# An encoder step on one core: norms from an all-ones product with roots on whole rows, and a written order for VectorE and ScalarE at the end

## The chip, the cores and the metric

The kernel runs on one core of a Trainium2 chip. The metric is device time in microseconds, and less is better. The core has a matrix engine (TensorE, PE in the profile, with its weight loads shown as PEld), VectorE (DVE), ScalarE (ACT), GpSimd (POOL) and a sync engine (SP) that issues transfers. TensorE writes its results to PSUM, from which VectorE and ScalarE read them. All other data of the kernel is in SBUF, as tiles of 128 partitions by some columns.

## What is computed

One inference step of a two-layer encoder over 512 prompt frames and 64 frames of a running stream, 576 tokens of 1024 features. Layer 0 mixes tokens by causal averages over 2 to 16 frames, layer 1 by sparse attention. Behind each mixer stands a perceptron (1024 to 4096 and back) with a squared ReLU. A root-mean-square norm stands ahead of each of these four parts, and one more at the end. Cut to what matters here:

```python
def _rmsnorm(x, g):
    xf = x.astype(jnp.float32)
    xf = xf * lax.rsqrt(jnp.mean(xf * xf, axis=-1, keepdims=True) + EPS)
    return (xf * g.astype(jnp.float32)).astype(x.dtype)

def _mlp(h, w_up, w_down):
    u = jax.nn.relu(h @ w_up)
    return (u * u) @ w_down

for i in range(DEPTH):
    h = _rmsnorm(x, norm_mix[i])
    ...
    x = x + y.astype(x.dtype)
    x = x + _mlp(_rmsnorm(x, norm_mlp[i]), w_up[i], w_down[i])
return _rmsnorm(x, norm_final)
```

## The kernel before, in words

**Layout.** The residual x lies transposed: eight tiles of 128 features (partitions) by 576 tokens (columns). A token's sum of squares therefore runs across partitions and across tiles. The 576 columns are two halves of 288 (`HT`). float32 products are made of two-part splits: every operand is an upper part and a lower part, and three products stand for one. The weights are split in the same way: a raw weight arrives by DMA, ScalarE casts it to the upper part `wh` (line 184), VectorE subtracts to get the lower part `wl` (line 185). One such pair is a unit of 512 columns; units lie in a ring of slots, and a cast into a slot waits until TensorE has read the slot's old content. `next_block` (line 248) asks for units some four to six ahead of their use.

**A perceptron's start.** `split_x` scales and splits x by the norm's gain, without the root, and `Norm.add` sums the squares of the eight tiles into `s2` (128 by 576). The up projection runs in blocks of 128 outputs (`project`, line 264): 48 products of 288 columns each, into a pair of PSUM banks. There are two such pairs. Since the root is a factor per token, it is applied when a block is read out: `activated` (line 373) takes max(block, 0) times `norm.rb`, the root spread over all partitions, into `v`. So the first two blocks need no norm; it has to be there before the fourth block can have the first block's banks. After the second block come the sums: `stats` (line 292) multiplies s2, 128 tokens at a time (the last time 64), with two columns of ones, so that token sums land one per partition, five columns in all, and `rms_steps` (line 330) turns them into inverse roots: a root on ScalarE, a reciprocal on VectorE, and one Newton step in three operations. During the third block (which has two single banks of its own) `spread` (line 297) puts them on all partitions: `diagonals` multiplies the identity with them on VectorE, a product with the all-ones block `ones` at k = 5 (`SPREAD_AT`) makes every partition hold every token's value in `rb`, and ScalarE copies that to `rbm` in SBUF (line 303). Then come the v's of the first two blocks (line 379).

**The end.** `last` (line 539) does the last two output tiles of the last perceptron (tiles 6 and 7) with plain products, one half of the tokens after the other, and puts the final norm beside them. `finish` (line 546) is a generator: token sums and roots, then the diagonal and its product, then the copy for GpSimd (which scales tiles 4 and 5), and then the scalings of all tiles (line 567) with the output DMAs. For the first half it is advanced at the feature steps 4, 11 and 13 (`NORM_STEPS`) of the second half's 16; for the second half it runs behind the last product. The second half's work on tiles 6 and 7 is an add to x (line 589), a square on ScalarE (line 591), and for tile 6 an add to the sum (line 593).

**What sets the order.** Each engine runs its own queue in order. Almost everywhere a scheduler of the framework orders each queue by its own model of the times; nothing in the code says when a `wl` comes relative to a `v`. Inside `tc.manual_schedule` (line 581) the engines named keep the order in which the code is written: before, TensorE alone. A semaphore holds an instruction until what it needs is there, and everything behind it on the same engine waits too.

Of the kernel before, what the change touches and what calls it, by code (L numbers as in the profile page):

```python
# [9 lines left out]
F32 = mybir.dt.float32  # L10
F32R = mybir.dt.float32r
AF = mybir.ActivationFunctionType
ALU = mybir.AluOpType
ENG = mybir.EngineType
PSUM = bass.MemoryType.PSUM

P = 128
D = 1024
KT = D // P
TP = 512  # L20
TS = 64
T = TP + TS
HT = T // 2
# [7 lines left out]
WARM = 16  # L31
LAST = 2
FINAL_ASIDE = ((4, 5), (4, 5))
NORM_STEPS = (4, 11, 13)
PACE = (1, 2, 2)
PACED = 3 * NIDX - 1
SLOTS = {"xs": 8, "a": 3, "b": 3, "c": 3, "d": 3, "e": 2}
HEADS = {"a": 512, "c": 1024, "d": 1024}
UNITS = (6, 2)
UNDER = 64  # L40
SPREAD_AT = 5
SPARE_UNITS = 6
RAWS = (2, 2)
MLP_BLOCKS = ("up", "even", "odd", "down")
# [6 lines left out]
def pool_dsa_kernel(ctx: ExitStack, tc: tile.TileContext, a, o):  # L51
# [30 lines left out]
    def slot(tag, s, dt=F32R):  # L82
        if tag == "x":
            return resid.tile([P, SLOT], dt, tag=tag, name=uid(s))
        n = HEADS.get(tag, SLOT) if "cst2" in phase else SLOT
        return phase["xs" if tag == "xs" else "slots"].tile([P, n], dt, tag=tag, bufs=SLOTS[tag], name=uid(s))
# [15 lines left out]
    def psum1(s="po"):  # L102
        return phase["po"].tile([P, 512], F32, tag="po", name=uid(s))
# [4 lines left out]
    def halves(t):  # L108
        return t.rearrange("p (h t) -> p h t", h=2)
# [154 lines left out]
    def project(pt, w, xs, between=iter(()), cols=((0, HT), (HT, HT))):  # L264

        n = len(xs)
        for k in range(n):
            next(between, None)
            wh, wl = at(w, k)
            for i, (wt, part) in enumerate(((wh, 0), (wh, 1), (wl, 0))):  # L270
                for h, (c, m) in enumerate(cols):
                    pe.matmul(  # L272
                        pt[h][:, :m] if isinstance(pt, tuple) else pt[:, h, :m], wt, xs[k][:, part, c:c + m],
                        start=(k == 0 and i == 0), stop=(k == n - 1 and i == 2),
                    )

    class Norm:
# [14 lines left out]
        def stats(self):  # L292
            pt = psum1("st")
            token_sums(pt, self.s2)
            self.r = rms(pt)

        def spread(self):
            diag = diagonals(self.r)
            self.rb = tmp("rb" + self.s, "rb", 1)
            for h in range(2):  # L300
                pb = psum1("rb")
                pe.matmul(pb[:, :HT], ones, diag[:, h * HT:(h + 1) * HT], start=True, stop=True)
                act.copy(self.rb[:, h * HT:(h + 1) * HT], pb[:, :HT])
            return self.rb

    def diagonals(r, n=T, diag=None):

        diag = tmp("diag") if diag is None else diag
        c, rest = n // P, n % P
        idb = ident.rearrange("p (o c) -> p o c", o=1)  # L310
        rc = r.rearrange("p (o c) -> p o c", c=1)
        dve.tensor_tensor(diag[:, :c * P].rearrange("p (i c) -> p i c", c=P), idb.to_broadcast([P, c, P]),
                          rc[:, :c].to_broadcast([P, c, P]), ALU.mult)
        if rest:
            dve.tensor_scalar(diag[:, c * P:n], ident[:, :rest], r[:, c:], None, ALU.mult)
        return diag

    def token_sums(pt, *sums, n=T):
        for i in range(0, n, P):
            m = min(P, n - i)  # L320
            for s2 in sums:
                pe.matmul(pt[:m, i // 64:i // 64 + 2], s2[:, i:i + m], ones[:, 0:2], start=s2 is sums[0], stop=s2 is sums[-1])

    def rms(pt, n=T):

        steps = rms_steps(pt, n)
        next(steps)
        return next(steps)

    def rms_steps(pt, n=T, early=False):  # L330
        c, rest = n // P, n % P
        ms, rt, t, r = (small(c + (rest > 0), s + str(n)) for s in ("ms", "rt", "nt", "r"))
        ends = [(P, slice(0, c), slice(0, 2 * c, 2))]
        if rest:
            dve.memset(ms[:, c:], 1.0)
            dve.memset(rt[:, c:], 1.0)
            ends.append((rest, slice(c, c + 1), slice(2 * c, 2 * c + 1)))
        if early:
            yield
        for rows, to, at in ends:  # L340
            act.activation(rt[:rows, to], pt[:rows, at], AF.Sqrt, scale=1.0 / D, bias=eps[:rows])
        for rows, to, at in ends:
            dve.tensor_scalar(ms[:rows, to], pt[:rows, at], 1.0 / D, EPS, ALU.mult, ALU.add)
        yield
        dve.reciprocal(r, rt)
        dve.scalar_tensor_tensor(t, r, -0.5, r, ALU.mult, ALU.mult)
        dve.tensor_tensor(t, t, ms, ALU.mult)
        dve.scalar_tensor_tensor(r, t, 1.5, r, ALU.add, ALU.mult)
        yield r
# [13 lines left out]
    def mlp(layer, gi, late=0, end=None):  # L363
# [127 lines left out]

        v = early = None

        def spread():

            for k in range(KT):
                if k == SPREAD_AT:
                    norm.spread()
                yield

        def finished(c, i, pt, us):
            nonlocal v, early
            if i % 2 == 0:
# [15 lines left out]
        for n, (c, i) in enumerate(steps):  # L519
            if i is not None:  # L520
                w = next_block()
                pt = (psum1("up"), psum1("up")) if n == 2 else psum("up")
                project(pt, w, xs, spread() if n == 2 else iter(()))
                todo.append((c, i, pt, us[c]))
                if n == 0:
                    continue
                if n == 1:
                    norm.stats()
                    continue
                for t in todo:  # L530
                    finished(*t)
                todo.clear()
                continue
            down(c, us[c])
# [4 lines left out]
    def last(parts):  # L539

        norm = Norm("f", lambda: slot("xs", "sq", F32)[:, :T])
        for k in range(KT - LAST):
            norm.add(k)
        ws = [next_block() for _ in range(LAST)]

        def finish(c, n, aside, rest):
            t = slice(c, c + n)
            room = halves(slot("xs", "room", F32))
            for k in aside:
                act.activation(x[k][:, t], x[k][:, t], AF.Copy, scale=gv[:, 4, k:k + 1])  # L550
            st = psum1("st")
            token_sums(st, norm.s2[:, t], rest, n=n)
            r = rms(st, n)
            yield
            diag = diagonals(r, n, room[:, 0])
            pb = psum1("rb")
            pe.matmul(pb[:, :n], ones, diag[:, :n], start=True, stop=True)
            yield
            if aside:
                rb = room[:, 1, :n]  # L560
                act.copy(rb, pb[:, :n])
            yield
            for k in range(KT):
                if k in aside:
                    pool.tensor_tensor(x[k][:, t], x[k][:, t], rb, ALU.mult)
                else:
                    dve.scalar_tensor_tensor(x[k][:, t], x[k][:, t], gv[:, 4, k:k + 1], pb[:, :n], ALU.mult, ALU.mult)
                if c and k > 3:
                    (nc.sync if k % 2 else act).dma_start(o["y"][:, k, t], x[k][:, t])
                elif k % 2:  # L570
                    nc.sync.dma_start(o["y"][:, k - 1:k + 1, t], x.t[k // 2][:, :, t])

        def during(steps):

            for k in range(LAST * KT):
                if k in NORM_STEPS:
                    next(steps)
                yield

        before = between = iter(())  # L580
        with tc.manual_schedule(engines={ENG.PE}):
            for c, n, us in ((0, HT, parts[0]), (HT, HT, parts[1])):
                t = slice(c, c + n)
                s2 = norm.s2[:, t]
                for j in range(LAST):
                    k = KT - LAST + j
                    pt = psum("dn")
                    project(pt, ws[j], us, between, cols=((0, n),))
                    dve.tensor_tensor(x[k][:, t], x[k][:, t], pt[:, 0, :n], ALU.add)
                    sq = norm.room()[:, :n]  # L590
                    act.activation(sq, x[k][:, t], AF.Square)
                    if j < LAST - 1:
                        dve.tensor_tensor(s2, s2, sq, ALU.add)
                for _ in before:
                    pass
                before = finish(c, n, FINAL_ASIDE[c > 0], sq)
                between = during(before)
            for _ in before:
                pass
# [735 lines left out]
```

## Time and profile before

| what | value |
|---|---|
| median of 3 runs (lowest to highest) | 1113.73 us (1112.39 to 1115.95) |
| span of the profiled execution, first to last instruction | 1114.1 us |
| busy share of TensorE, VectorE, ScalarE, GpSimd | 98%, 74%, 48%, 27% |
| mean granted TensorE clock | 0.991 |
| first and second perceptron: token sums start | 56.4 us, 724.0 us |
| end: first half's sums start; last six scalings start | 1092.3 us, 1106.6 us |

Profile rows are read like this: start and duration in us, engine, line, operation, output tile <- input tiles, shape, count, and in brackets how long the engine sat idle before, and what ended that. A product of plain float32 operands shows as two entries, so "x4" at line 302 is two products. The span of 1114.1 us is 0.4 above the median of the runs.

### The profile page before, as it was taken

The numbers are of one execution on the slowest core, as the hardware profiler recorded it, in microseconds if no ns is written. First come the engines' busy times: TensorE is split into PE (matmuls) and PEld (weight loads), VectorE is DVE, ScalarE is ACT, GpSimd is POOL, SyncE is SP. The second block draws the span as 40 slices with busy tenths as digits, with TensorE's granted clock in tenths as the row PEclk, the third lists the DMA queues.
The fourth block names the chain that finished last, engine by engine and source line by source line (L and its number), as shares of the span: only waits on it lengthen the run. The fifth ranks groups of instructions, "written<-read, shape, count | busy, mean of one in ns | idle before, by whom it ended". The sixth has DMA issues, their size and how long they took to land.

```text
span 1114.1 us, 21065 instructions
## 1 busy us (share of the span) xinstructions
PE 1090.9 (98%) x8222; PEld 1077.3 (97%) x8222; DVE 825.7 (74%) x1562; ACT 539.0 (48%) x983; POOL 305.1 (27%) x260
## 2 busy tenths in 40 slices
PE   8999999999999999999899999999999999999995
PEld 8999999999999999999889999999999999999995
DVE  7867856866786797779799954767757866766884
ACT  8545434434434454443387665545434434434541
POOL 3312201302221261227682430012211302231331
PEclk8999999999999999999999999999999999999997
DMA  6433542554365345446742443643643554365212
GB/s 218 138 104 77 160 135 77 122 162 114 86 161 142 77 128 178 117 150 178 204 115 66 137 116 112 173 117 77 161 133 85 123 153 114 86 164 140 57 39 85
DMA packets 60610, 138.72 MB, mean 125 GB/s; under 512 B 9969, under 2 KB 21536, under 8 KB 60512
## 3 DMA queue, kind: packets, MB, share of 16 engines
q1 hardware_dynamic: 46544, 103.50, 30.4%
q0 software_dynamic: 8928, 16.26, 9.2%
q10 hardware_dynamic: 5040, 17.63, 5.2%
q8 instruction: 65, 1.06, 0.4%
q14 instruction: 33, 0.27, 0.1%
HBM read 122.28 MB, written 10.89 MB: 120 GB/s over the span
## 4 chain that ended last, share of the span: by engine, by line
PE 82%; DVE 10%; DMA 3%; ACT 1%; issue 1%; SPq 1%; POOL 0%; DVEq 0%; ACTq 0%; POOLq 0%
PE up L272 37%; PE b L439 13%; PE c L439 8%; PE a L439 8%; PE wo L272 3%; PE pj L272 2%; DVE work L1016 2%; DVE m L1015 2%; DMA raw<-in_w_in 2%; PE o L1091 2%; PE z L702 2%; PE pb L807 1%; PE wa L272 1%; DVE wl L185 1%; PE dn L272 1%
## 5 line engine op out<-in xcount | busy, mean ns | idle before, releaser
L272 PE MATMUL up<-xs,wh 128*128 128x288 f32 x2048 | 355.5, 295 | 0.0
L184 ACT CAST wh<-raw 128x512 fp32r<-128x512 f32 (+1 forms) x316 | 194.1, 620 | 303.2 <-PE up L272 130.6
L272 PEld LDWEIGHTS up<-xs,wh 128*128 128x128 f32 x2048 | 299.6, 188 | 0.6 <-DVE v L379 0.4
L185 DVE TENSOR_TENSOR wl<-raw,wh 128x512 fp32r<-128x512 f32 (+1 forms) x292 | 235.6, 810 | 63.6 <-ACT wh L184 58.6
L272 PE MATMUL up<-xs,wl 128*128 128x288 f32 x1024 | 218.6, 295 | 0.0
L272 PEld LDWEIGHTS up<-xs,wl 128*128 128x128 f32 x1024 | 164.0, 188 | 0.0
L439 PE MATMUL b<-u,wh 128*128 128x288 f32 x744 | 150.1, 295 | 0.2 <-DVE x L484 0.2
L439 PEld LDWEIGHTS b<-u,wh 128*128 128x128 f32 x744 | 119.0, 188 | 0.5 <-DVE x L484 0.5
L226 POOL TENSOR_TENSOR sum<-sum,raw 128x512 f32<-128x512 f32 x31 | 52.9, 1708 | 241.3 <-DMA raw<-in_w_down 187.9
L184 ACT CAST wh<-sum 128x512 fp32r<-128x512 f32 x93 | 56.9, 620 | 110.1 <-PE up L272 42.8
L439 PE MATMUL b<-u,wl 128*128 128x288 f32 x372 | 109.0, 295 | 0.0
L439 PE MATMUL a<-u,wh 128*128 128x288 f32 x496 | 101.2, 295 | 0.0
L439 PE MATMUL c<-u,wh 128*128 128x288 f32 x496 | 100.4, 295 | 0.0
L379 DVE SCALAR_TENSOR_TENSOR v<-up,rbm 128x576 f32<-128x576 f32 x60 | 45.2, 756 | 66.7 <-PE up L272 62.4
L185 DVE TENSOR_TENSOR wl<-sum,wh 128x512 fp32r<-128x512 f32 x93 | 76.9, 830 | 7.6 <-ACT wh L184 6.3
L439 PEld LDWEIGHTS a<-u,wh 128*128 128x128 f32 x496 | 79.6, 188 | 0.0
L439 PEld LDWEIGHTS c<-u,wh 128*128 128x128 f32 x496 | 79.3, 188 | 0.1
L209 POOL DMA_DIRECT2D raw<-in_w_down x31 | 26.8, 866 | 185.0 <-DMA raw<-in_w_down 89.3
L439 PE MATMUL a<-u,wl 128*128 128x288 f32 x248 | 73.2, 296 | 0.1
L439 PE MATMUL c<-u,wl 128*128 128x288 f32 x248 | 73.0, 294 | 0.0
L439 PEld LDWEIGHTS b<-u,wl 128*128 128x128 f32 x372 | 69.7, 188 | 0.0
L208 POOL DMA_DIRECT2D sum<-in_w_down x31 | 28.4, 934 | 141.4 <-DVE wl L185 85.1
(246 smaller groups left out, 2010.0 us busy)
## 6 DMA issues: line engine op xcount, KB each, us to landing
raw<-in_w_up SPq DMA_DIRECT2D x64, 512.0 KB, 3.8
raw<-in_w_down SPq DMA_DIRECT2D x64, 512.0 KB, 3.6
raw<-in_w_o ACTq DMA_DIRECT2D x16, 512.0 KB, 3.8
sum<-in_w_down SPq DMA_DIRECT2D x31, 256.0 KB, 3.9
sum<-in_w_down POOLq DMA_DIRECT2D x31, 256.0 KB, 5.2
raw<-in_w_down POOLq DMA_DIRECT2D x31, 256.0 KB, 4.1
raw<-in_w_in ACTq DMA_DIRECT2D x15, 512.0 KB, 4.4
q<-st SPq DMA_DIRECT2D x32, 144.0 KB, 2.5
```

The costliest lines, as they stand in the source:

```text
L184: act.copy(h, src)
L185: how["sub"].tensor_tensor(l, src, f32(h), ALU.subtract)
L208: pool.dma_start(s1, odd[:, 512:], accum_op=ALU.add)
L209: pool.dma_start(raw[:, :512], even[:, :512], accum_op=ALU.add)
L226: pool.tensor_tensor(s2, s1, a11, ALU.add)
L272: pe.matmul(pt[h][:, :m] if isinstance(pt, tuple) else pt[:, h, :m], wt, xs[k][:, part, c:c + m], start=(k == 0 and i == 0), stop=(k == n ...
L379: dve.scalar_tensor_tensor(v, pt[:, :, :HT], 0.0, halves(norm.rb), ALU.max, ALU.mult)
L439: pe.matmul(bank[:, :HT], wt, ut, start=first and j == 0 and i == 0, stop=last and j == 3 and i == 2, skip_group_check=True)
L702: pe.matmul(z[s, i][:n, (g % 2) * 256:(g % 2 + 1) * 256], lhs, rhs, start=kk + j == 0, stop=kk == 1 and j == 2)
L1015: dve.max(m8[:np_], wk[:np_])
L1016: dve.match_replace(wk[:np_], m8[:np_], wk[:np_], TAKEN)
L1091: pe.matmul(oc[:, 2 * s + hh], pT[:, c:c + P], V[:, kt, vs], start=kt == 0, stop=kt == i)
```

## The change

In the perceptrons, one function `everywhere` takes the place of `stats` and `spread`. For each half it multiplies the all-ones block with the squares' sum s2, so that every partition gets every token's sum at once, and makes the inverse root on the full 128 by 288 block by `root`: a root on ScalarE, then on VectorE a reciprocal and three operations of the Newton step. There are no diagonal, no second product and no copy. It is called behind the second block, where `stats` was. The generator that put the spread into the third block goes.

The last norm does the same on each half (two products into one bank, s2 and the last square), at step 4; the root lies in PSUM, where the scalings read it. The scalings of the first half are written in three parts: tiles 0 and 1 with the root, 2 to 5 at step 8, 6 and 7 behind the second half's last add. The gain scalings of GpSimd's tiles move behind the root on ScalarE. And in this last part VectorE and ScalarE, too, keep the written order. The norm ahead of the attention stays as it was; `rms_steps` and `diagonals` only lose a parameter (not shown).

```diff
-NORM_STEPS = (4, 11, 13)
+NORM_STEPS = (4, 8)
-SPREAD_AT = 5
...
+        def everywhere(self):
+            self.rb = tmp("rb" + self.s, "rb", 1)
+            for h in range(2):
+                t = slice(h * HT, (h + 1) * HT)
+                pt = psum1("st")
+                pe.matmul(pt[:, :HT], ones, self.s2[:, t], start=True, stop=True)
+                root(self.rb[:, t], pt[:, :HT], self.rb[:, t], tmp("nt")[:, :HT])
...
+    def root(r, sums, first, t):
+        act.activation(t, sums, AF.Sqrt, scale=1.0 / D, bias=eps)
+        dve.reciprocal(first, t)
+        dve.scalar_tensor_tensor(t, first, -0.5 / D, first, ALU.mult, ALU.mult)
+        dve.scalar_tensor_tensor(t, sums, D * EPS, t, ALU.add, ALU.mult)
+        dve.scalar_tensor_tensor(r, t, 1.5, first, ALU.add, ALU.mult)
...
-                project(pt, w, xs, spread() if n == 2 else iter(()))
+                project(pt, w, xs)
...
-                    norm.stats()
+                    norm.everywhere()
...
         def finish(c, n, aside, rest):
             t = slice(c, c + n)
-            room = halves(slot("xs", "room", F32))
+            room = slot("xs", "room", F32)
+            first, spare, rb = (room[:, i * n:(i + 1) * n] for i in range(3))
+            pb = psum1("rb")
+            pe.matmul(pb[:, :n], ones, norm.s2[:, t], start=True, stop=False)
+            pe.matmul(pb[:, :n], ones, rest, start=False, stop=True)
+            root(pb[:, :n], pb[:, :n], first, spare)
             for k in aside:
                 act.activation(x[k][:, t], x[k][:, t], AF.Copy, scale=gv[:, 4, k:k + 1])
-            st = psum1("st")
-            token_sums(st, norm.s2[:, t], rest, n=n)
-            r = rms(st, n)
-            yield
-            diag = diagonals(r, n, room[:, 0])
-            pb = psum1("rb")
-            pe.matmul(pb[:, :n], ones, diag[:, :n], start=True, stop=True)
-            yield
-            if aside:
-                rb = room[:, 1, :n]
-                act.copy(rb, pb[:, :n])
-            yield
+            act.copy(rb, pb[:, :n])
             for k in range(KT):
+                if k in (2, 6):
+                    yield
                 if k in aside:
                     pool.tensor_tensor(x[k][:, t], x[k][:, t], rb, ALU.mult)
...
-        with tc.manual_schedule(engines={ENG.PE}):
+        with tc.manual_schedule(engines={ENG.PE, ENG.DVE, ENG.Activation}):
```

How this moves the queues, at the places where it matters. VectorE at the first perceptron's start, before (st holds the token sums, r the roots; wl_959 and wl_963 are the subtractions for the two halves of a later block's weights; v is the readout of the first two blocks):

```order
L343 TENSOR_SCALAR ms_128_782<-st_776 128x4
L343 TENSOR_SCALAR ms_128_782<-st_776 64x1
L345 RECIPROCAL r_131_785<-rt_129_783 128x5
L346 SCALAR_TENSOR_TENSOR nt_130_784<-r_131_785 128x5
L347 TENSOR_TENSOR nt_130_784<-nt_130_784,ms_128_782 128x5
L348 SCALAR_TENSOR_TENSOR r_131_785<-nt_130_784,r_131_785 128x5
L312 TENSOR_TENSOR diag_838<-ident,r_131_785 128x512
L315 TENSOR_SCALAR diag_838<-ident,r_131_785 128x64
L185 TENSOR_TENSOR wl_959<-raw_796,wh_958 128x512
L379 SCALAR_TENSOR_TENSOR v_866<-up_678,rbm_140_841 128x576
L379 SCALAR_TENSOR_TENSOR v_866<-up_727,rbm_140_841 128x576
L185 TENSOR_TENSOR wl_963<-raw_796,wh_962 128x512
```

The same place of the changed kernel, where the lines and numbers are a little lower (wl_946 is the old wl_959, wl_950 the old wl_963; nt and rbm are the two halves' roots):

```order
L317 RECIPROCAL rbm_127_776<-nt_779 128x288
L317 RECIPROCAL rbm_127_776<-nt_787 128x288
L318 SCALAR_TENSOR_TENSOR nt_779<-rbm_127_776 128x288
L184 TENSOR_TENSOR wl_946<-raw_793,wh_945 128x512
L318 SCALAR_TENSOR_TENSOR nt_787<-rbm_127_776 128x288
L319 SCALAR_TENSOR_TENSOR nt_779<-st_777,nt_779 128x288
L319 SCALAR_TENSOR_TENSOR nt_787<-st_785,nt_787 128x288
L320 SCALAR_TENSOR_TENSOR rbm_127_776<-nt_779,rbm_127_776 128x288
L320 SCALAR_TENSOR_TENSOR rbm_127_776<-nt_787,rbm_127_776 128x288
L184 TENSOR_TENSOR wl_950<-raw_793,wh_949 128x512
L395 SCALAR_TENSOR_TENSOR v_853<-up_678,rbm_127_776 128x576
L395 SCALAR_TENSOR_TENSOR v_853<-up_727,rbm_127_776 128x576
```

Eight operations on all 288 columns stand where eight smaller ones stood, wl_946 has come in between them, and wl_950, which stood behind the v's, now stands ahead of them. The second perceptron has the same sequence.

VectorE at the end, before (x_8384 is tiles 6 and 7, dn_13030 and dn_13083 the second half's products for them, rb_13095 the first half's root, s the sum of squares):

```order
L348 SCALAR_TENSOR_TENSOR r_2081_13056<-nt_2080_13055,r_2081_13056 128x3
L589 TENSOR_TENSOR x_8384<-x_8384,dn_13030 128x288
L312 TENSOR_TENSOR room_13043<-ident,r_2081_13056 128x256
L315 TENSOR_SCALAR room_13043<-ident,r_2081_13056 128x32
L593 TENSOR_TENSOR s_2065_12954<-s_2065_12954,sq_13080 128x288
L567 SCALAR_TENSOR_TENSOR x_8381<-x_8381,gv,rb_13095 128x288 x2
L567 SCALAR_TENSOR_TENSOR x_8382<-x_8382,gv,rb_13095 128x288 x2
L567 SCALAR_TENSOR_TENSOR x_8384<-x_8384,gv,rb_13095 128x288 x2
L589 TENSOR_TENSOR x_8384<-x_8384,dn_13083 128x288
```

The same place of the changed kernel (x_8371 is tiles 6 and 7, dn_13004 and dn_13048 the products, rb_13018 the first half's root):

```order
L317 RECIPROCAL room_13017<-room_13017 128x288
L318 SCALAR_TENSOR_TENSOR room_13017<-room_13017 128x288
L319 SCALAR_TENSOR_TENSOR room_13017<-rb_13018,room_13017 128x288
L320 SCALAR_TENSOR_TENSOR rb_13018<-room_13017 128x288
L572 SCALAR_TENSOR_TENSOR x_8368<-x_8368,gv,rb_13018 128x288 x2
L594 TENSOR_TENSOR x_8371<-x_8371,dn_13004 128x288
L598 TENSOR_TENSOR s_2057_12928<-s_2057_12928,sq_13045 128x288
L572 SCALAR_TENSOR_TENSOR x_8369<-x_8369,gv,rb_13018 128x288 x2
L594 TENSOR_TENSOR x_8371<-x_8371,dn_13048 128x288
L572 SCALAR_TENSOR_TENSOR x_8371<-x_8371,gv,rb_13018 128x288 x2
```

The add of dn_13004 (tile 6), which stood ahead of the diagonal, now stands behind the whole root and two scalings; the add of dn_13048 (tile 7), which stood behind all six scalings, now stands ahead of the last two.

More of the change, by code (lines that the diff above doesn't have):

```diff
@@ L304, in spread, with diagonals @@
             return self.rb
-    def diagonals(r, n=T, diag=None):
-        diag = tmp("diag") if diag is None else diag
-        c, rest = n // P, n % P
+    def root(r, sums, first, t):
[4 more added lines that the diff above has]
+        dve.scalar_tensor_tensor(r, t, 1.5, first, ALU.add, ALU.mult)
+    def diagonals(r):
+        diag = tmp("diag")
+        c, rest = T // P, T % P
         idb = ident.rearrange("p (o c) -> p o c", o=1)
@@ L314, in diagonals, with token_sums, rms, rms_steps @@
         if rest:
-            dve.tensor_scalar(diag[:, c * P:n], ident[:, :rest], r[:, c:], None, ALU.mult)
+            dve.tensor_scalar(diag[:, c * P:], ident[:, :rest], r[:, c:], None, ALU.mult)
         return diag
-    def token_sums(pt, *sums, n=T):
-        for i in range(0, n, P):
-            m = min(P, n - i)
+    def token_sums(pt, *sums):
+        for i in range(0, T, P):
+            m = min(P, T - i)
             for s2 in sums:
                 pe.matmul(pt[:m, i // 64:i // 64 + 2], s2[:, i:i + m], ones[:, 0:2], start=s2 is sums[0], stop=s2 is sums[-1])
-    def rms(pt, n=T):
-        steps = rms_steps(pt, n)
+    def rms(pt):
+        steps = rms_steps(pt)
         next(steps)
         return next(steps)
-    def rms_steps(pt, n=T, early=False):
-        c, rest = n // P, n % P
-        ms, rt, t, r = (small(c + (rest > 0), s + str(n)) for s in ("ms", "rt", "nt", "r"))
+    def rms_steps(pt, early=False):
+        c, rest = T // P, T % P
+        ms, rt, t, r = (small(c + (rest > 0), s) for s in ("ms", "rt", "nt", "r"))
         ends = [(P, slice(0, c), slice(0, 2 * c, 2))]
@@ L492, in mlp @@
         v = early = None
[L494 to L498, printed above, removed]
-                yield
         def finished(c, i, pt, us):
@@ L547, in finish @@
             t = slice(c, c + n)
-            room = halves(slot("xs", "room", F32))
+            room = slot("xs", "room", F32)
[4 more added lines that the diff above has]
+            root(pb[:, :n], pb[:, :n], first, spare)
             for k in aside:
                 act.activation(x[k][:, t], x[k][:, t], AF.Copy, scale=gv[:, 4, k:k + 1])
-            st = psum1("st")
-            token_sums(st, norm.s2[:, t], rest, n=n)
-            r = rms(st, n)
-            yield
-            diag = diagonals(r, n, room[:, 0])
-            pb = psum1("rb")
-            pe.matmul(pb[:, :n], ones, diag[:, :n], start=True, stop=True)
-            yield
-            if aside:
-                rb = room[:, 1, :n]
-                act.copy(rb, pb[:, :n])
-            yield
+            act.copy(rb, pb[:, :n])
             for k in range(KT):
+                if k in (2, 6):
+                    yield
                 if k in aside:
```

## The prediction, made before the changed kernel ran

> **What bounds the kernel now.** I read the page first, then the timelines of three places (the start of each perceptron, the end), then the groups with shapes kept apart, for the operation that the change enlarges.
>
> ```profile
> span 1114.1 us, 21065 instructions
> PE 1090.9 (98%) x8222; PEld 1077.3 (97%) x8222; DVE 825.7 (74%) x1562; ACT 539.0 (48%) x983; POOL 305.1 (27%) x260
> PE 82%; DVE 10%; DMA 3%; ACT 1%; issue 1%; SPq 1%; POOL 0%; DVEq 0%; ACTq 0%; POOLq 0%
> ```
>
> TensorE is busy in 98% of the span and 82% of the chain that ended last. So what counts is whether TensorE waits, and what happens after its last product. The first perceptron's start, in time order:
>
> ```profile
> 56.42 1.15 PE L322 MATMUL st<-ones,s 128*128 128x2 f32 x10
> 57.06 0.69 DVE L185 TENSOR_TENSOR wl<-raw,wh 128x512 fp32r<-128x512 f32 x1 [2.51 <-ACT wh L184]
> 58.13 0.42 PE L272 MATMUL up<-xs,wl 128*128 128x288 f32 x2
> 60.74 0.62 ACT L184 CAST wh<-raw 128x512 fp32r<-128x512 f32 x1 [2.72 <-issue]
> 62.61 1.14 PE L302 MATMUL rb<-diag,ones 128*128 128x288 f32 x4
> 63.30 0.89 ACT L303 COPY rbm<-rb 128x288 f32<-128x288 f32 x2 [1.94 <-PE rb L302]
> 63.85 0.42 PE L272 MATMUL up<-xs,wl 128*128 128x288 f32 x2
> 64.11 0.70 PE L272 MATMUL up<-xs,wh 128*128 128x288 f32 x4
> 64.22 1.42 DVE L379 SCALAR_TENSOR_TENSOR v<-up,rbm 128x576 f32<-128x576 f32 x2 [2.13 <-ACT rbm L303]
> 64.64 0.43 PE L272 MATMUL up<-xs,wl 128*128 128x288 f32 x2
> 64.90 0.62 ACT L184 CAST wh<-raw 128x512 fp32r<-128x512 f32 x1 [0.71 <-PE up L272]
> 65.03 0.56 PEld L272 LDWEIGHTS up<-xs,wh 128*128 128x128 f32 x4 [0.19 <-DVE v L379]
> 65.56 0.68 DVE L185 TENSOR_TENSOR wl<-raw,wh 128x512 fp32r<-128x512 f32 x1
> 66.16 0.45 DVE L397 TENSOR_TENSOR t<-v 128x288 f32<-128x288 f32 x1
> ```
>
> Two blocks of the up projection are done at 56.42 and hold both PSUM pairs. The third uses spare banks; the fourth needs the first pair back, which VectorE's first v (64.22) reads out. TensorE goes on at 65.03, 0.81 us after v started, having waited 0.19 us. So the norm has the third block's time to get ready, and today it just does not need more.
>
> **The first perceptron.** Four products of the block take 64.64 - 64.11 = 0.53 us, 0.13 each. The first pair of wl products, at 58.13, stands behind four others, so the token sums held TensorE 58.13 - 0.53 - 56.42 = 1.18 us. The two products for rb held it from 62.61 to 0.26 before 63.85, 0.98 us. The change removes both and puts two products of the second form where the sums were: the third block ends 1.18 us earlier, at 63.72 instead of 64.90. That is the gain, if nobody waits.
>
> In place of six operations on five columns stand, for each half, a root on ScalarE and a reciprocal and three more operations on VectorE, all on 288 columns. The rows nearest to a long reciprocal:
>
> ```profile
> L345 DVE RECIPROCAL r<-rt 128x5 f32<-128x5 f32 x4 | 0.7, 171 | 0.0
> L345 DVE RECIPROCAL r<-rt 128x3 f32<-128x3 f32 x2 | 0.3, 154 | 0.0
> L347 DVE TENSOR_TENSOR nt<-nt,ms 128x5 f32<-128x5 f32 x4 | 0.7, 166 | 0.1
> L347 DVE TENSOR_TENSOR nt<-nt,ms 128x3 f32<-128x3 f32 x2 | 0.3, 161 | 0.1
> L1116 DVE RECIPROCAL rs<-sums x3: 169/177/178, 629.5 to 649.1; 128x4 f32<-128x4 f32 x3
> L1116 DVE RECIPROCAL rs<-sums x4: 166/166/166, 656.8 to 678.3; 128x2 f32<-128x2 f32 x4
> L550 ACT ACTIVATE x<-x,gv 128x288 f32<-128x288 f32 x4 | 1.9, 530 | 0.1
> 69.04 0.82 DVE L377 SCALAR_TENSOR_TENSOR v<-up,rbm 128x288 f32<-128x288 f32 x2
> ```
>
> Two more columns make a reciprocal 17 ns longer and a plain product only 5. At 8.5 ns a column, 288 columns take 171 + 283 x 8.5 = **2.58 us**. Two rows of another line (medians 177 for four columns, 166 for two) give 5.5 ns a column and 1.74 us. The low end is that of any other pass over 288 columns, 0.45 us (two take 0.82, the second starting 0.37 after the first). I take 2.58, from the row with most columns, and keep 0.45 and 1.74. The Trainium skill (VectorE: DVE Perf Modes, the section on the TRN2 errata) prices a VectorE operation at 58 cycles plus one per column at 0.96 GHz; as an estimate from that page the reciprocal would take 0.36 us, and the total would be that of the third rival below. The 17 ns for two columns speak against it.
>
> Now VectorE's queue, in the order that the section on the change shows. The subtraction at 57.06 stays; the next operation may start 0.60 later (65.56 to 66.16), at 57.66. The sums are readable 0.69 after their first product, as for rb (62.61 to 63.30), so at 57.11; the root takes 0.53 (the two-operand row of ScalarE) and is out at 57.64. First reciprocal 57.66; a following independent operation starts 0.09 before the former's end, so the second at 60.15, and VectorE is free at 62.64. One product 0.37: 63.01. The subtraction for wl_946, whose cast (60.74, now some 0.2 earlier) is long done, 0.60: 63.61. Five products of 0.37: 65.46. Then the subtraction for **wl_950**, 0.60: 66.06. Only then the first v, and TensorE 0.81 later: **66.87 against 65.03, +1.84 us**. The third block now ends at 63.72, so TensorE stands still for 3.1 us.
>
> wl_950 has a price of its own. Its cast waits for the end of the third block (64.90 in the rows), its subtraction follows 0.65 later, and the first v, which used to go ahead of it, is now queued behind it. Even with a reciprocal at no cost, TensorE could not go on before 63.72 + 0.64 + 0.60 + 0.81 = 65.77, which is +0.74. Behind v wait its squares on ScalarE, the factors, and TensorE's fourth block.
>
> **The second perceptron** has the same queues:
>
> ```profile
> 724.65 0.69 DVE L185 TENSOR_TENSOR wl<-raw,wh 128x512 fp32r<-128x512 f32 x1 [2.47 <-ACT wh L184]
> 732.65 0.56 PEld L272 LDWEIGHTS up<-xs,wh 128*128 128x128 f32 x4 [0.20 <-DVE v L379]
> ```
>
> From the subtraction to TensorE were 8.00 us; with the new queue 66.87 - 57.06 = 9.81: **+1.81**. TensorE has no slack behind either place to take this up, so both count in full: +3.65.
>
> **The end.**
>
> ```profile
> 1092.27 0.28 PE L322 MATMUL st<-ones,s 128*128 128x2 f32 x2
> 1095.27 0.45 DVE L589 TENSOR_TENSOR x<-x,dn 128x288 f32<-128x288 f32 x1 [0.48 <-PE dn L272]
> 1095.75 0.45 ACT L591 ACTIVATE sq<-x 128x288 f32<-128x288 f32 x1 [1.89 <-DVE x L589]
> 1097.48 2.64 DVE L567 SCALAR_TENSOR_TENSOR x<-x,gv,rb 128x288 f32<-128x288 f32 x6 [0.79 <-ACT room L561]
> 1098.71 0.29 PE L272 MATMUL dn<-u,wl 128*128 128x288 f32 x1
> 1104.78 1.33 PE L557 MATMUL rb<-room,ones 128*128 128x288 f32 x2 [2.02 <-DVE room L315]
> 1106.14 0.40 ACT L561 COPY room<-rb 128x288 f32<-128x288 f32 x1 [2.94 <-PE rb L557]
> 1106.57 2.64 DVE L567 SCALAR_TENSOR_TENSOR x<-x,gv,rb 128x288 f32<-128x288 f32 x6 [1.85 <-ACT room L561]
> ```
>
> Here VectorE is the chain. The last six scalings start at 1106.57, and from there to the end little changes: the output DMAs keep their order on SP and ScalarE. In these times, without the shift above: the two products start at 1092.27 and are readable 0.69 + 0.49 later (the second copy at 63.30 starts 0.49 after the first), 1093.45; root 0.53; a handover of 0.04 at each step from here (the copies end at 64.19, v starts at 64.22). Reciprocal 1094.02 to 1096.64; three dependent products of 0.49: 1098.11. Two scalings of 0.44 (2.64 for six): 1098.99. The add of tile 6 now comes here, in the order written, not at 1095.27: 1099.48; its square 1099.97; the sum 0.37: 1100.34; two scalings: 1101.22; the add of tile 7: 1101.71 (its product was ready near 1099.0, so TensorE is not what it waits for); its square: 1102.20. The product takes 1.36 until it can be read (1104.78 to 1106.14): 1103.56. Root: 1104.13. Reciprocal: 1106.75. Three products: 1108.22. **+1.65 us** against 1106.57. What is saved here is real (sums, small operations, a second product, the copy ahead of the scalings) and the two reciprocals, 5.2 us in series, eat it. The scalings by gain on ScalarE, moved behind the root, take twice 0.53 under a reciprocal of 2.58; uncovered they would add 1.0. The copy for GpSimd's two tiles runs beside VectorE's scalings.
>
> Eight memsets go at the kernel's start, before the inputs have arrived: nothing, at most a gain of eight times 0.17 (the length of any tiny row above), 1.4 us. Order on GpSimd and SP is unchanged.
>
> **The clock.** So far 3.65 + 1.65 = +5.3 us. The stalls of 3.1 us have a second price:
>
> ```profile
> 19.01:22.42 3.41, 2.74 (x13) 2.64 (x13) 2.94 (x18) 3.04 (x7) 0.00 (x0) 0.50 0.46 138
> 22.42:25.83 3.41, 3.41 (x18) 3.41 (x17) 3.36 (x7) 3.32 (x8) 1.46 (x2) 0.50 0.09 35
> 551.49:554.90 3.41, 1.98 (x14) 1.54 (x14) 0.98 (x8) 1.97 (x7) 3.41 (x4) 1.00 0.80 290
> 1097.62:1101.03 3.41, 1.51 (x14) 1.43 (x12) 2.86 (x7) 0.44 (x1) 1.48 (x2) 1.00 0.51 179
> 1101.03:1104.45 3.42, 1.73 (x10) 1.63 (x10) 1.08 (x7) 0.40 (x2) 0.00 (x0) 0.50 0.47 167
> ```
>
> The first column of numbers is TensorE's busy time, the third from the right its granted clock. After 3.41 us with 1.51 busy the clock was halved; after 3.41 with 1.98 busy it was not. A stall of 3.1 us leaves less than 1.5 busy in most positions of such a stretch. A drop costs half of its length while there is work: between nothing and 3.4 us (the drop at 19.0 lasted 6.8). I take a drop half that long, with some 0.8 of its 3.4 us still in the stall: 1.3 us, twice, +2.6. The Trainium skill (TensorE: Matmul & The Clock Gate, What's actually happening) has the clock fall after an idle window of about 3.4 us; by that a stall of 3.1 would not do it, which is the first rival. The row with 1.51 us busy is against so strict a reading.
>
> **How the numbers follow.** The sum stands on the profiled span of 1114.1, 0.4 above the median of 1113.73; I add to the median.
> - Forecast, **0.42**: 5.3 + 2.6 = 7.9, **1121.6 us**.
> - First rival, the clock holds, 0.25: +5.3, 1119.0. For it: no drop between 26 and 1101 us.
> - Second rival, the reciprocal takes 1.74, 0.13: VectorE is through before wl_950's cast, so +0.74 twice, and the end comes out 0.1 earlier by the same steps: 1115.1.
> - Third rival, not slower: the reciprocal costs what any pass does, 0.45, 0.12. It is decided in the queue at the end: two reciprocals shorter by 2.13 bring the last scalings 2.7 earlier than before (1103.87), against +1.5 in the perceptrons: -1.2, 1112.5. Below about 1.0 us for a reciprocal the change pays.
> - 0.05 for drops as long as the one at 19.0 (5.3 + 6.8 and more, from 1125.8 up), 0.03 that the perceptrons' stall does not come about.
>
> The range leaves out the third rival, the longest drops and the last case, 0.20 together: 1115.0 to 1125.8. A measurement of this kernel tells about 0.3%, 3.3 us, from no change. Slower by more: 0.42 + 0.25 + 0.05 and 0.03 of the second rival with a drop, 0.75. Within: 0.10 + 0.10 + 0.01 = 0.21. Faster by more: 0.04, the rest of the third rival and of the last case.
>
> **What would show it.** A reciprocal of 288 columns near 2.58 us; TensorE waiting some 3 us for v, once in each perceptron, with VectorE's subtraction for wl directly ahead of v; a granted clock of 0.5 in the 3 to 7 us behind; in the end, the last six scalings 15.9 us behind the first product for the last norm's sums (1092.27 to 1108.22), where it was 14.3. I am wrong if the reciprocal comes out under 1 us, or if v starts before the third block is done.

## The result, and the profile after

| | before | after |
|---|---|---|
| median (lowest to highest), 4 runs each | 1113.06 us (1112.1 to 1115.95) | 1121.16 us (1118.22 to 1123.25) |
| span of the profiled execution | 1114.1 us | 1116.1 us |

The changed kernel is slower: the medians differ by 8.1 us. The ratio of the times is 1.0064, with a 95% interval of 1.0044 to 1.0084, which stands for 7.1 us (4.9 to 9.4). The two spans differ by only 2.0 us, and that is no contradiction. The profiled execution of the changed kernel was its fastest (1118.22, 2.1 more than its span). That of before, with the same 2.1 added, lies near 1116, at its slowest. Part of that lies ahead of the first perceptron, whose token sums start at 56.42 us before and at 54.56 after; in the kernels of the experiments that start is anywhere between 54.21 and 56.36. So the spans aren't subtracted here; the traces are read place by place.

The head of the page after, and the first line of its chain:

```profile
span 1116.1 us, 20965 instructions
PE 1087.7 (97%) x8182; PEld 1073.0 (96%) x8182; DVE 840.0 (75%) x1546; ACT 538.9 (48%) x977; POOL 304.1 (27%) x260
PE 82%; DVE 10%; DMA 3%; issue 2%; ACT 1%; SPq 1%; POOL 0%; DVEq 0%; ACTq 0%; POOLq 0%
```

TensorE has 3 us less to do and VectorE 14 us more, and the chain looks as before. The loss is seen only where an engine waits. In TensorE's list of waits (total, times, longest) a new line stands on top:

```profile
PE up L271 <- DVE v L395: 4.9, 2, 2.8
```

Before, these two waits were 0.19 and 0.20 us. The timeline of the first perceptron's start, of several engines, in order of time:

```profile
54.56 0.89 PE L302 MATMUL st<-s,ones 128*128 128x288 f32 x3
55.84 3.76 DVE L317 RECIPROCAL rbm<-nt 128x288 f32<-128x288 f32 x2
59.52 0.40 DVE L318 SCALAR_TENSOR_TENSOR nt<-rbm 128x288 f32<-128x288 f32 x1
59.78 1.28 POOL L225 TENSOR_TENSOR sum<-sum,raw 128x512 f32<-128x512 f32 x1 [19.63 <-DMA raw<-in_w_down]
59.83 1.78 DVE L184 TENSOR_TENSOR wl<-raw,wh 128x512 fp32r<-128x512 f32 x1
63.37 0.68 DVE L184 TENSOR_TENSOR wl<-raw,wh 128x512 fp32r<-128x512 f32 x1
63.97 1.41 DVE L395 SCALAR_TENSOR_TENSOR v<-up,rbm 128x576 f32<-128x576 f32 x2
64.86 0.76 PE L271 MATMUL up<-xs,wh 128*128 128x288 f32 x4 [2.84 <-DVE v L395]
```

From the sums to TensorE's next block: 64.86 - 54.56 = 10.30 us, where it was 65.03 - 56.42 = 8.61: **+1.69**. Two things were not as I had them. The two reciprocals are shorter than I took (3.68 us from the first's start to the next operation, 59.52 - 55.84; I had 4.98). And the subtraction between the Newton products took 1.78 us, where the same operation in the line below took 0.68. Beside it runs an addition on GpSimd.

The second perceptron's start, with the token sums of before as the first line:

```profile
724.02 1.16 PE L322 MATMUL st<-ones,s 128*128 128x2 f32 x10
722.58 0.89 PE L302 MATMUL st<-s,ones 128*128 128x288 f32 x3
727.82 0.68 DVE L184 TENSOR_TENSOR wl<-raw,wh 128x512 fp32r<-128x512 f32 x1
728.43 1.60 POOL L225 TENSOR_TENSOR sum<-sum,raw 128x512 f32<-128x512 f32 x1 [31.48 <-DMA raw<-in_w_down]
729.51 1.20 DVE L320 SCALAR_TENSOR_TENSOR rbm<-nt,rbm 128x288 f32<-128x288 f32 x2
732.13 1.05 PE L271 MATMUL up<-xs,wh 128*128 128x288 f32 x4 [2.08 <-DVE v L395]
```

GpSimd's addition came 0.6 us behind the subtraction's start, and only the two last products were longer (1.20 instead of some 0.82). Here the way is 9.55 us against 8.63 before (724.02 to 732.65): **+0.92**.

The windows around both waits, cut where the clock can change (TensorE's busy time first, its granted clock third from the right):

```profile
59.99:63.40 3.41, 2.03 (x16) 1.79 (x14) 3.41 (x7) 0.62 (x1) 1.89 (x2) 1.00 0.26 35
63.40:66.82 3.42, 1.96 (x15) 1.99 (x16) 3.13 (x7) 2.04 (x3) 0.00 (x0) 1.00 0.67 180
729.00:732.42 3.42, 1.33 (x10) 1.14 (x10) 3.42 (x7) 1.02 (x2) 1.82 (x2) 1.00 0.31 34
732.42:735.83 3.41, 3.41 (x16) 3.41 (x15) 3.08 (x7) 3.01 (x4) 0.00 (x0) 0.50 0.69 199
```

The first wait was split between two windows, 2.03 and 1.96 us busy remained in them, and the clock held. The second lay in one; 1.33 us busy remained, and the next window ran at half clock. At half speed 3.41 us of work lose up to 1.7 us. From this block to the end's first product for the sums are 361.05 us (732.13 to 1093.18), before 359.62 (732.65 to 1092.27): **+1.43** is what the halved window cost.

The end, in order of time:

```profile
1093.18 0.65 PE L560 MATMUL rb<-s,ones 128*128 128x288 f32 x2
1101.12 1.33 PE L560 MATMUL rb<-s,ones 128*128 128x288 f32 x2 [2.04 <-DVE s L598]
1104.71 1.95 DVE L317 RECIPROCAL room<-room 128x288 f32<-128x288 f32 x1 [1.58 <-ACT room L316]
1108.18 0.40 ACT L565 COPY room<-rb 128x288 f32<-128x288 f32 x1 [2.66 <-DVE rb L320]
1108.61 2.64 DVE L572 SCALAR_TENSOR_TENSOR x<-x,gv,rb 128x288 f32<-128x288 f32 x6 [0.47 <-ACT room L565]
```

First product for the sums to last scalings: 15.43 us, before 14.30: **+1.13**. The scalings wait 0.47 us for ScalarE's copy of the root, which reads the same PSUM bank; why the two are put in order no run tests.

### The profile page after: what moved, and what is told of

Read it like the earlier page. It is cut to its first block, busy times and chain, and to the rows that moved or that the text cites. A ratio compares the mean times of both kernels' runs of the same rounds, so it can differ in the third digit from the quotient of the medians.

```text
span 1116.1 us, 20965 instructions
## 1 busy us (share of the span) xinstructions
PE 1087.7 (97%) x8182; PEld 1073.0 (96%) x8182; DVE 840.0 (75%) x1546; ACT 538.9 (48%) x977; POOL 304.1 (27%) x260
## 4 chain that ended last, share of the span: by engine, by line
PE 82%; DVE 10%; DMA 3%; issue 2%; ACT 1%; SPq 1%; POOL 0%; DVEq 0%; ACTq 0%; POOLq 0%
PE up L271 35%; PE b L455 12%; PE c L455 8%; PE a L455 8%; PE pj L271 6%; PE wo L271 3%; DVE wl L184 2%; PE o L1096 2%; DMA raw<-in_w_in 1%; PE pb L812 1%; PE wa L271 1%; DVE work L1021 1%; DVE m L1020 1%; PE sc L1057 1%; DVE p L1035 1%
```

## The experiments

Each kernel ran beside the kernel before on the same chip, in three sets. In the set with the two parts apart, the subtractions on GpSimd and the product for the reciprocal, the median of before was 1113.48 us; with the held addition, the cleared queue and the root on ScalarE 1112.61; with the filled wait 1113.28.

**The two places apart.** First only the perceptrons' part of the change: `everywhere` and `root` added to the kernel before, its old `finish` and order kept.

```diff
-                project(pt, w, xs, spread() if n == 2 else iter(()))
+                project(pt, w, xs)
...
-                    norm.stats()
+                    norm.everywhere()
```

> The perceptrons' norms as changed, the last norm and its written order as before. Theory (the loss is mainly TensorE's two waits for v and the halved clock behind them): the waits cost 1.69 and 0.92 us between the profiles, each halved clock window behind a wait 1.7 us (3.41 us at 0.5), one or two of them: 1113.1 + 2.6 + 1.7 to 3.4 = 1117.4 to 1119.1 us, up to 1120 if this edit holds all that the end does not. Rival (the end's new order holds the larger part): the waits alone, 1115.7 us or less, and no window of 0.5 behind them that the kernel before lacks.

Measured: 1118.06 us, ratio 1.0044 (1.0029 to 1.0060), so 4.6 us. Both waits are there (5.6 us in all), and each lies for the most part in one window. Its windows:

```profile
62.16:65.57 3.41, 1.00 (x8) 1.03 (x9) 3.32 (x7) 1.14 (x3) 0.03 (x1) 1.00 0.75 94
65.57:68.98 3.41, 3.41 (x17) 3.41 (x16) 3.17 (x8) 2.30 (x3) 0.66 (x1) 0.50 0.35 137
731.17:734.58 3.41, 1.17 (x9) 1.20 (x10) 3.22 (x7) 1.28 (x2) 0.00 (x0) 1.00 0.68 119
734.58:737.99 3.41, 3.41 (x17) 3.41 (x16) 3.27 (x7) 2.14 (x3) 0.86 (x1) 0.50 0.27 112
```

As the theory had it, with two halved windows. Which of an execution's waits is followed by one depends on where it falls in the row of windows.

Then only the end: the new `finish`, its steps and the written order of VectorE and ScalarE, with the old norms in the perceptrons.

```diff
-NORM_STEPS = (4, 11, 13)
+NORM_STEPS = (4, 8)
...
-        with tc.manual_schedule(engines={ENG.PE}):
+        with tc.manual_schedule(engines={ENG.PE, ENG.DVE, ENG.Activation}):
```

> The last norm and the written order as changed, the perceptrons' norms as before. Theory: the end costs 1.13 us, as between the profiles (last norm's first product of sums to the last scalings 15.43 us against 14.30): 1114.2 us. Rival (the end holds the larger part of the 8.1 us, by work that the written order moves outside of that stretch): 1117 us or more.

Measured: 1115.59 us, ratio 1.0025 (1.0014 to 1.0036), 2.1 us. That is between the two expectations: 1 us more than the trace accounts for, and I have not found where it goes. This run's own trace has the same 15.43 us at the end (1089.98 to 1105.41). The parts, 4.6 and 2.1, come to 6.7, which fits the 8.1 of the whole within the intervals. By the medians the larger part is the perceptrons'.

**What makes v late: first try.** The two subtractions go to GpSimd.

```diff
-                w = next_block()
+                w = next_block(pool if n == 4 else dve)
```

> The change, with the subtractions of wl_946 and wl_950 (and of their two fellows in the second perceptron) on GpSimd in place of VectorE; the reciprocals stay. Theory A (what makes v late is the queue on VectorE: the subtraction between the Newton products, 1.78 us beside GpSimd's addition in the first perceptron and 0.68 in the second, and the one ahead of v, 0.6 each): v comes 2.4 and 1.3 us earlier, TensorE's waits of 2.8 and 2.1 us shrink to 0.4 and 0.8, and no window is halved behind them: 1121.2 - 3.7 - 1.7 to 3.4 = 1114.1 to 1115.8 us. Theory B (the reciprocals and Newton's products are the chain, the subtractions only fill its gaps): under 1 us gained, 1120.2 us or more. Rival on the clock (the halved window behind the second wait came by chance): 1117.5 us.

Measured: 1121.59 us, ratio 1.0079 (1.0062 to 1.0097): nothing gained. The number is theory B's, but the trace shows another thing. The first perceptron's start, of GpSimd and VectorE and then TensorE:

```profile
61.30 1.56 POOL L225 TENSOR_TENSOR sum<-sum,raw 128x512 f32<-128x512 f32 x1 [19.28 <-DMA raw<-in_w_down]
61.32 1.85 DVE L318 SCALAR_TENSOR_TENSOR nt<-rbm 128x288 f32<-128x288 f32 x2
62.82 1.49 POOL L184 TENSOR_TENSOR wl<-raw,wh 128x512 fp32r<-128x512 f32 x1
63.10 0.81 DVE L319 SCALAR_TENSOR_TENSOR nt<-st,nt 128x288 f32<-128x288 f32 x2
63.83 2.93 DVE L320 SCALAR_TENSOR_TENSOR rbm<-nt,rbm 128x288 f32<-128x288 f32 x2
64.87 1.56 POOL L184 TENSOR_TENSOR wl<-raw,wh 128x512 fp32r<-128x512 f32 x1
67.69 1.30 PE L271 MATMUL up<-xs,wh 128*128 128x288 f32 x4 [3.87 <-DVE v L395]
```

Two products of this shape take some 0.81 us. The pairs at 61.32 and 63.83 took 1.85 and 2.93, and end 0.3 us behind the GpSimd operations that run beside them (62.86, 66.43). The pair at 63.10 was beside one too and took 0.81. The difference: lines 318 and 320 read two operands from SBUF, line 319 reads one from PSUM. The Trainium skill (SBUF — State Buffer, SBUF: two separate sides) states this: VectorE and GpSimd share one pair of ports under an exclusive lock, which a VectorE operation with two SBUF inputs needs, and whoever comes second waits for the whole of the other's instruction. The rows here agree. So the move exchanged two subtractions for 3.2 us of holding (1.85 + 2.93 - 2 x 0.81). TensorE waited 3.87 us in the first perceptron, and its clock was halved for two windows.

**The collision by itself.** GpSimd's addition is held back until v: a one-column copy from v, overwritten at once, goes ahead of it. VectorE's order stays.

```diff
+            if "v" in how:
+                pool.tensor_copy(s2[:, :1], how.pop("v")[:, 0, :1])
             pool.tensor_tensor(s2, s1, a11, ALU.add)
...
```

> The change, with GpSimd's first addition in each perceptron held back until v (a one-column copy from v into its tile ahead of it, overwritten by the addition); VectorE's, ScalarE's and TensorE's orders are those of the change. Theory (a VectorE instruction that reads two operands from SBUF and starts beside GpSimd's addition is held until that ends: in the change the subtraction took 1.78 us for 0.68, in the run with the old end a product 1.54 for 0.45): the held instruction goes back to its own length, v comes 1.1 and about 0.4 us earlier, TensorE waits 1.7 us twice, no window falls to half: 1121.2 - 1.5 - 1.7 to 3.4 = 1116.1 to 1118.0 us. Rival (the long rows are VectorE's own: a subtraction behind reciprocals, whatever GpSimd does): the row of 1.1 us too much stays, 1121 us.

Measured: 1116.32 us, ratio 1.0033 (1.0020 to 1.0045). VectorE and GpSimd at the first start, and TensorE's next block:

```profile
60.48 0.68 DVE L184 TENSOR_TENSOR wl<-raw,wh 128x512 fp32r<-128x512 f32 x1
64.66 0.77 PE L273 MATMUL up<-xs,wh 128*128 128x288 f32 x4 [1.99 <-DVE v L397]
65.86 1.29 POOL L227 TENSOR_TENSOR sum<-sum,raw 128x512 f32<-128x512 f32 x1
65.92 1.54 DVE L416 TENSOR_TENSOR t<-v,t 128x288 f32<-128x288 f32 x1 [0.20 <-ACT v L398]
```

The subtraction is back at 0.68 us, and the hold has gone with the addition to the next VectorE operation with two SBUF operands, a 0.46 us one that now takes 1.54 and that TensorE does not wait for. The rival is out. TensorE waits 2.0 us twice, more than the 1.7 expected, and behind the second wait (1.48 us busy in its window) the clock was still halved, against the expectation; the time is at the lower end of the expected range all the same. From the sums to TensorE's next block are 9.45 us in the first perceptron (55.21 to 64.66) and 9.40 in the second (722.29 to 731.69): +0.84 and +0.77 against before.

**The queue as well.** The two subtractions are held behind v too, by the same means.

```diff
+        if how.get("behind"):
+            dve.tensor_copy(l[:, :1], how["last"][:, 0, :1])
         how["sub"].tensor_tensor(l, src, f32(h), ALU.subtract)
...
```

> As the run before, and the two subtractions of wl_946 and wl_950 (and their fellows in the second perceptron) held behind v on VectorE too (a one-column copy from v, overwritten). Between the sums and v are then the two roots, the two reciprocals and six products alone. Theory (queue, collision and reciprocals add up): v starts 3.7 + 6 x 0.37 us behind the first reciprocal's start, TensorE waits 0.7 to 0.9 us twice, against 1.24 us of its own work that the change takes out of each perceptron: perceptrons 0.4 us each below the kernel before, the end 1.7 to 2.1 above: 1113.5 - 0.9 + 1.9 = 1114.5 us, give or take 0.8. Rival (the subtractions fill gaps between dependent products and cost nothing): like the run with the addition alone held back, 1116 us or more.

Measured: 1112.71 us, ratio 1.0003 (0.9991 to 1.0016): no difference from before. The first start:

```profile
55.49 3.77 DVE L321 RECIPROCAL rbm<-nt 128x288 f32<-128x288 f32 x2
60.58 0.82 DVE L324 SCALAR_TENSOR_TENSOR rbm<-nt,rbm 128x288 f32<-128x288 f32 x2
61.43 1.42 DVE L399 SCALAR_TENSOR_TENSOR v<-up,rbm 128x576 f32<-128x576 f32 x2
62.34 0.77 PE L275 MATMUL up<-xs,wh 128*128 128x288 f32 x4 [0.66 <-DVE v L399]
```

TensorE waits 0.66 us (1.3 for both), less than the work that the change takes off it there, and no window is halved. Even with its reciprocals the new norm would cost the perceptrons nothing, if nothing stood in its queue. From the sums to TensorE's next block are 8.13 and 8.09 us (54.21 to 62.34 and 719.27 to 727.36), 0.48 and 0.54 less than before; with the 1.13 that the end takes longer this comes to +0.1, as measured. The time is 1.8 us under the expectation, which took 1113.5 for the kernel before (0.9 above this set's) and priced the end at 1.9.

**The reciprocal.** A product with a constant in its place, so that the norms are a guess and not the true ones:

```diff
...
-        dve.reciprocal(first, t)
+        dve.scalar_tensor_tensor(first, t, 0.0, guess, ALU.mult, ALU.add)
```

> The change, with each reciprocal of a row replaced by a scalar_tensor_tensor of the same shape with a constant tile, so that the root is a guess and not the root; with that the scheduler also puts both v ahead of the two subtractions. Theory: each reciprocal takes 1.95 us and its stand-in 0.45, so 3.0 us less in each perceptron, more than the waits of 2.8 and 2.1 there: TensorE runs through them and no window is halved; at the end 2 x 1.5 = 3.0 less than with the change, 1.9 less than before. Sum 1113.1 - 1.9 = 1111.2 us. Rival (other parts of the change, the sums by an all-ones block or the roots on whole rows from PSUM, carry the loss): 1116 us or more.

Measured: 1108.15 us, ratio 0.9957 (0.9940 to 0.9973). TensorE does not wait for v at all. With the shorter operation the scheduler also puts both v's ahead of the two subtractions, so the queue changes with the price. The time is 3 us below the expectation; most of that is that TensorE saves 1.2 us of work in each perceptron, which the expectation had left out and which counts when nobody waits, and the end took 2.4 us less than before (11.86 against 14.30), not 1.9. So the whole loss, and a gain behind it, hang on the reciprocals and what they push.

**A root without the reciprocal.** ScalarE makes the inverse root itself, in every norm of the kernel, and Newton's step stays:

```diff
-        act.activation(t, sums, AF.Sqrt, scale=1.0 / D, bias=eps)
-        dve.reciprocal(first, t)
+        act.activation(first, sums, AF.Abs_reciprocal_sqrt, scale=1.0 / D, bias=eps)
...
```

> The change, with ScalarE's square root and VectorE's reciprocal replaced by one ScalarE activation of the reciprocal square root (every norm, so that one table of functions serves), and Newton's step on it as before. Theory (the 1.95 us of each reciprocal carry the whole loss): like the run with products in their place, less those products: perceptrons without a wait, 1.24 us each below the kernel before; the end 2 x 0.4 below that run: 1108.2 - 0.8 = 1107.4 us. Rival (the gain of that run came from its data, whose norms were not the roots: granted clock or otherwise; or the other function costs ScalarE more than the root's 0.50 us): 1110 us or more.

Measured: 1108.17 us, ratio 0.9959 (0.9941 to 0.9977): **faster than both kernels**, by 4.4 us than the one before, and 0.8 above the expectation. It is the same time as with the products, now with the true norms, so the data of that run played no part. In the groups by shape, the new activation, and in the timeline the end:

```profile
L316 ACT ACTIVATE rbm<-st,eps 128x288 f32<-128x288 f32 x4 | 2.0, 502 | 0.2
```

```profile
1093.73 0.75 PE L558 MATMUL rb<-s,ones 128*128 128x288 f32 x2
1095.42 0.75 PE L559 MATMUL rb<-sq,ones 128*128 128x288 f32 x2 [0.94 <-ACT sq L594]
1098.66 2.64 DVE L570 SCALAR_TENSOR_TENSOR x<-x,gv,rb 128x288 f32<-128x288 f32 x6 [0.47 <-ACT room L563]
```

It costs ScalarE what the square root did (502 ns against 501). From TensorE's sums of the second half to the last scalings are 4.9 us, with the change 1108.61 - 1101.12 = 7.5 (its products there ran at half clock, 1.33 for 0.75, which is some 0.6 of the difference: with the wait filled, the next experiment, they ran at full clock and the way took 6.92); and the 2.04 us wait ahead of those sums is gone, since that was for a VectorE add queued behind the first half's reciprocal.

**The clock by itself.** Seven products that nobody uses fill TensorE's wait; v stays as late as it was.

```diff
...
+                if n == 2:
+                    for _ in range(7):
+                        pe.matmul(norm.st[:, :P], ones, ones, start=True, stop=True)
```

> The change, with seven products of the all-ones block by itself on TensorE at the place where it waits for v in each perceptron (into the bank of the sums, which is read by then; their results are used by nobody). Nothing else moves on any engine, and v comes as late as before. Theory (a stretch of 3.41 us in which TensorE is busy for less than about half halves its clock in the next, and that is a cost of the wait beside the wait itself): no window behind either wait falls to half, and the time is 1.7 us per window saved below the change's: 1121.2 - 1.7 to 2.4 = 1118.8 to 1119.5 us. Rival (the halved window behind the second wait has nothing to do with the wait's idle time): a window of 0.5 within 7 us of a wait is still there, 1121 us.

Measured: 1118.59 us, ratio 1.0049 (1.0033 to 1.0065). TensorE at the second wait, and the windows there:

```profile
732.55 1.83 PE L538 MATMUL st<-ones 128*128 128x128 f32 x14 [0.71 <-DVE nt L321]
734.65 0.76 PE L272 MATMUL up<-xs,wh 128*128 128x288 f32 x4 [0.27 <-DVE v L397]
```

```profile
729.39:732.80 3.41, 2.70 (x21) 2.47 (x20) 3.41 (x8) 0.62 (x1) 2.21 (x2) 1.00 0.20 25
732.80:736.21 3.41, 3.14 (x26) 2.98 (x26) 3.12 (x7) 1.64 (x3) 0.00 (x0) 1.00 0.64 163
```

The wait is as long as it usually is (0.71 + 1.83 + 0.27 = 2.81 us), and no window behind either wait is halved, as the theory had it. But this execution alone does not prove it: the wait happened to be split between two windows. Without the seven products these would still have had 2.45 and 1.56 us of work (0.25 and 1.58 of the 1.83 us fell into them), while the drops behind idle time that these traces show have at most 1.51 ahead of them (the prediction's row at 1097.62); at the first wait it would have been 2.2 and 1.75. The times don't decide it either: 5.3 us above its before, where the change was 8.1 above its own, is 2.8 us less, but the two intervals overlap.

What ties the halved clock to the waits is the comparison across the traces. From the second wait's end to the end's first product for the sums are 361.04 to 361.10 us in the three kernels with a halved window there (the change, the perceptrons alone, the held addition), and 359.47 to 359.62 in the four without one (before, the subtractions on GpSimd, the cleared queue, the filled wait). Each of the three had 1.17 to 1.48 us of work in the window of the wait, the others 1.8 or more.

## Why the prediction was right

The direction came out, and so did the chain that was forecast: long reciprocals in VectorE's queue, wl_950 ahead of v, a wait of TensorE in each perceptron, a halved clock behind some of them, a longer end. That the sum came within half a microsecond (1121.6 us predicted, 1121.16 measured) is luck. The reciprocal was priced too high, and with its measured price alone the prediction's own steps give 0.74 twice and 0.39 at the end, 1115.6 us and a clock term on top. A collision with GpSimd, which the prediction does not know, and the scalings' wait for ScalarE's copy at the end put a good part of the difference back.

- **Reciprocal, taken at 2.58 us: 1.95.** In the changed kernel's groups by shape (count, total us, mean ns, idle before):

```profile
L317 DVE RECIPROCAL rbm<-nt 128x288 f32<-128x288 f32 x4 | 7.5, 1923 | 0.0
L317 DVE RECIPROCAL room<-room 128x288 f32<-128x288 f32 x2 | 3.9, 1953 | 4.2 <-ACT room L316 4.2
```

From 5 columns (170 ns) to 288 (1953) that is 6.3 ns a column; the two rows that I had extended gave 8.5 and 5.5. It lies nearer to the second rival's 1.74, but that rival's time of 1115.1 did not come: its +0.74 in each perceptron shows only where the collision is out of the way (+0.84 and +0.77 with the addition held).
- **First perceptron, +1.84: +1.69.** A right sum of wrong parts. The reciprocals were 1.3 us shorter, and the collision with GpSimd, of which the prediction knows nothing, put 1.1 back (1.78 instead of 0.68). With the reciprocal alone corrected my steps give +0.74, the wait for wl_950's cast.
- **Second perceptron, +1.81: +0.92 in the profiled execution,** where GpSimd's addition came later and hit less. In two other kernels with the same queue the second wait was 2.80 and 2.81 us, not 2.08, so the profiled one was short.
- **The end, +1.65: +1.13 in the trace,** 2.1 by the run of the end alone. The reciprocals took 1.26 less than I had, and the scalings' wait for ScalarE's copy, which I had passed as running beside them, added some 0.4 in each half. A row of before had shown that wait: the scalings at 1106.57 follow ScalarE's copy, which ends at 1106.54.
- **Clock, two drops of 1.3: right in kind.** One drop that cost 1.43 us in the profiled execution, two drops in the run of the perceptrons alone. The first rival, that the clock holds through a 3 us wait, is right for the first wait of the profiled execution, which was split between two windows, and wrong for its second and for both in the run of the perceptrons alone.
- **wl_950 ahead of v** has its price: with the collision gone the perceptrons lose the +0.74 that was derived from it (+0.84 and +0.77), and taking it out of the queue together with wl_946 moved the ratio from 1.0033 to 1.0003; no run moves wl_950 alone. That even a free reciprocal would leave +0.74 there was not tested with the order kept: with the product in its place the scheduler put v ahead of wl_950 again, and the time fell to 1108.15, not to the 1112.5 of the third rival. That rival's sign was right: the reciprocal's price decides.

The profile's terms come to 1.69 + 0.92 + 1.13 + 1.43 = 5.2 us. A usual second wait adds 0.7, and one more halved window in some executions 1.4. That makes 5.9 to 7.3, against 7.1 by the ratio (4.9 to 9.4) and 8.1 by the medians. What is left by the medians is within the noise, and no run shows where it would lie: the run of the end alone was 1 us longer than its trace accounts for, the run with the cleared queue was not.

## What to carry to other kernels

Fewer operations are no gain if one of the new ones is long and stands ahead of a readout that TensorE waits for; price it at its full width, and then see which short operations the scheduler now puts between it and the readout. A wait of TensorE costs more than its length when it leaves a window of its clock with little work. And an operation that suddenly takes three times as long is a reason to look at what the neighbouring engine started just before it.

## What the runs showed of the hardware

- A VectorE operation with two SBUF operands that starts while a GpSimd one runs is held until that ends (1.78 us for 0.68, 1.54 for 0.46, a pair beside two of them 2.93 for 0.81); with one operand in PSUM it is not held (0.81 for a pair beside a 1.49 us GpSimd operation).
- Around these waits TensorE's clock changed on a fixed grid of 3.41 us (59.99 and 729.00 in the changed kernel lie 196 such windows apart). It was halved behind windows with 0.49 to 1.48 us of work, and held behind windows with 1.81 and more. The Trainium skill (TensorE: Matmul & The Clock Gate, What's actually happening) describes such a free-running window, which these traces show; it names an idle window as the condition, and here a window that was busy for two fifths was enough. Work is not all that counts: early in the kernel before, the window from 19.01 was halved although TensorE had been busy for all of the one ahead of it (15.60 to 19.01).
- Coming back took work as well. In the run with the subtractions on GpSimd, a halved window with 2.46 us of work was followed by another halved one; behind that one, with 3.41 us, the clock was full again:

```profile
66.74:70.15 3.41, 2.46 (x10) 2.49 (x11) 3.09 (x8) 2.27 (x3) 0.00 (x0) 0.50 0.70 194
70.15:73.56 3.41, 3.41 (x16) 3.41 (x15) 3.06 (x5) 1.32 (x2) 0.87 (x1) 0.50 0.20 25
```
